# A hybrid state-space and attention block: squares added feature-major, Toeplitz taps from SBUF, bias tiles that stay

## The chip, the cores and the metric

The kernel runs on one core of one Trainium2 chip. The metric is the device time of one execution in microseconds (us), as the median of several runs. A core has a matrix engine (PE; its weight loads are listed apart, as PEld), a vector engine (DVE), a scalar engine (ACT), a general-purpose engine (POOL) and a sync engine (SP) which here only issues transfers. The engines run their own instruction queues in order and wait for each other through semaphores. Sixteen DMA engines move data between DRAM and SBUF, the on-chip memory; PE writes its products into PSUM, eight banks from which the other engines read.

## What is computed

The input is x, 2048 tokens by 1024 features, in float32. The reference, cut to what the change touches:

```python
h = rmsnorm(x, norm_mix_g)              # x * rsqrt(mean(x*x, over features) + eps) * g
proj = h @ w_in                         # 1024 -> 512 (u) + 512 (q) + 512 (k) + 512 (v)
# group A: 32 channel groups of 16, one 64-dim diagonal complex state each
lam_bar = exp(lam * dt);  b_bar = ((lam_bar - 1) / lam)[..., None] * b_mat
states = scan(a_r * b_l + b_r over time, b_bar applied to u)
y_ssm = Re(C states) + d_skip * u;  y_ssm = glu(gelu(y_ssm))
# group B: 8 heads of 64; each 64-frame chunk looks at itself and the 8 chunks before
idx = clip(rel, -128, 128) + 128;  bias = rel_bias[:, idx]
out = softmax(q k^T / 8 + bias, invalid chunks at -1e30) @ v
x = x + concat(rmsnorm(y_ssm), rmsnorm(out)) @ w_out
x = x + (silu(h2 @ w_gate) * (h2 @ w_up)) @ w_down          # h2 = rmsnorm(x)
return rmsnorm(x)
```

Three things in it matter below. The normalisation of the first projection needs, for each token, the sum of its squared features. The recurrence of group A is done in stretches of 8 time steps: inside a stretch it is a small Toeplitz matrix, whose entries ("taps", Re(C lam_bar^k B) for k = 0..7, with d_skip added at k = 0) are made from the parameters inside the kernel. The bias of a head depends on the distance alone, so a tile of 128 query rows by 640 keys is one row of 768 values, shifted by one per query row, with two 64 by 64 corners that mark keys out of reach.

## The kernel before

The program runs through five phases: a first stage (`u_phase`), attention with the state-space units woven in (`att_phase`, `ssm_unit`), the output projection (`mix_phase`), and the feed-forward layer (`gate_up_phase`, `down_phase`). Products are made to float32 accuracy from float32r halves: an operand is split into a rounded part `hi` and a rest `lo`, and each product is three matmuls (`mm3`).

**First stage.** It computes u = h @ w_in[:, :512] in four blocks of 512 tokens, in the order 1, 2, 3, 0 (`BLOCKS`); we call these turns n = 0 to 3. For each block `prep` loads eight feature-major tiles `xt` of 128 features by 512 tokens (L441, four buffers), makes `hi` on ACT (L443, with the gain folded in) and `lo` on DVE (L444). It then loads the same tokens once more, token-major, as four tiles of 128 by 1024 (L450), and ACT squares each and adds along its row (L451); the four sums per token tile go to a Newton iteration on DVE (`newton`, L102 to L113, thirteen small instructions), started in `sums`. A `group` is one output tile of 128 features by 512 tokens: 24 matmuls. The scale of block n-1 is applied in turn n behind its first group: `finish` spreads the reciprocal roots over the partitions with PE (`spread_`, eight matmul records into a PSUM bank called `pp`), ACT copies them out (L473, L477, L478), DVE multiplies the four held groups (L483) and POOL sends them to DRAM (L484). A held group keeps its PSUM bank until then.

**The state-space prologue.** `ssm_prologue` is a generator; `long(n)` in `u_phase` advances it n steps, and `LONG = 1, 3, 2` says how many in each turn. It computes powers of lam_bar and b_bar, then four pieces `v` on DVE (L283 to L287), each of which POOL sends to DRAM (L345) with its state rows for the two channel groups of a pair lying in different halves of the 128 partitions. The other operand goes to DRAM as well (`bb`, L335). Both are read back regrouped, so that real and imaginary part of one channel group fill the 128 partitions (`bbg` L372, `vg`/`v` L379, 512 KB each), and 32 matmuls over 128 rows (L389) give the taps, four matmuls per PSUM bank; ACT copies them out (L390), DVE adds the diagonal (L392), POOL writes them to `kts` (L393). A chain of small complex multiplications on POOL (L356 to L365) makes the powers `a8`, `sw` for the scan. Last come 32 transposes of `wt` (L289 to L298), whose results ACT copies out (L295) and POOL sends to DRAM (`bsts`). These last parts are yielded into the first attention projection.

**Attention.** The phase is a list of 128 steps which a planner fills with the projection work of later blocks. The first step needs q and k of head pair 0 (`qk(0,0)`, 48 matmuls), made ready by ACT, DVE and a copying transfer (L750, L751). Each step multiplies q and k into a PSUM tile `sc`, DVE adds the bias tile `nb` and takes the row maximum in one instruction (L830), ACT takes the exponential, PE transposes the result (`pt`) and multiplies it with v. Bias tiles come from a DRAM array `nbm` of 8 heads by 128 by 640, built once by one 2.56 MB transfer and two transfers for the corners (L522, L525); `load_nb` (L799 to L802) loads one head's tile into one of two buffers. A state-space unit loads its operands `U`, `Bst`, `Tm`, `Vm` in 18 transfers (L550), multiplies on PE (`pj`), and scans on POOL.

All `dma_start` calls written `nc.sync` stand in SP's queue, those written `nc.gpsimd` in POOL's; a queue issues in program order, so a transfer whose semaphore wait is not fulfilled holds back the ones after it. In SP's queue each issue also waits until the transfer eight places earlier has landed, as there are eight semaphores in turn.

Of the kernel before, what the change touches and what calls it, by code (L numbers as in the profile page):

```python
# [65 lines left out]
LONG = 1, 3, 2  # L66
# [91 lines left out]
def ssm_prologue(k, ident, S):  # L158
# [3 lines left out]
    with tc.tile_pool(name="pro", bufs=1) as p:  # L162
# [126 lines left out]
        def transposes(b_, wt):  # L289
            bst = k.t(p, "v" if b_ > 1 else "vg", [P, 9 if b_ > 1 else 8, 2, NS], bufs=2)[:, :8]  # L290
# [46 lines left out]
        wts = []  # L337
        for b_ in range(4):
            qs = slice(4 * b_, 4 * b_ + 4)
# [27 lines left out]
        kt = k.t(p, "kt", [CH, 8, P], bufs=2)  # L367
        nc.gpsimd.memset(kt[:], 0.0)
        for b_ in range(4):
            nc.gpsimd.dma_start(S["kt"][:, 8 * b_ : 8 * b_ + 8, 0], kt[:])  # L370
        bb = k.t(p, "bbg", [P, NG, CH])
        nc.sync.dma_start(bb[:], S["bb"].rearrange("q g c n m -> (c n) (q g) m"))  # L372
        dm = k.t(p, "cm1", [P, 576])[:CH, : NG * CH].rearrange("c (g m) -> c g m", g=NG)
        V.tensor_tensor(dm, ident[:CH, :CH].unsqueeze(1).to_broadcast([CH, NG, CH]),
                        ddt[:].unsqueeze(2).to_broadcast([CH, NG, CH]), op=ALU.mult)
        vgs = []
        for b_ in range(4):
            vgs.append(k.t(p, "vg", [P, 8, P], bufs=2)[:] if b_ < 2 else k.t(p, "v", [P, 9, P], bufs=2)[:, :8])
            nc.sync.dma_start(vgs[b_], S["v"].rearrange("q g c n m -> (c n) (q g) m")[:, 8 * b_ : 8 * b_ + 8, :P])  # L379
        for b_ in range(4):  # L380
            gs = slice(8 * b_, 8 * b_ + 8)
            vg = vgs[b_]
            kt = k.t(p, "kt", [CH, 8, P], bufs=2) if b_ < 2 else k.t(p, ("bc", "small")[b_ - 2], [CH, 8, P])
            if b_ == 0:
                yield
            for g0 in (0, 4):
                ps = k.t(k.pro_psum, "pp", [P, 512])[:].rearrange("p (a b) -> p a b", a=4)
                for g in range(4):
                    k.te.matmul(ps[:CH, g, :], bb[:, 8 * b_ + g0 + g, :], vg[:, g0 + g, :], start=True, stop=True)  # L389
                nc.scalar.copy(kt[:, g0 : g0 + 4, :], ps[:CH])  # L390
                yield
            V.tensor_tensor(kt[:, :, :CH], kt[:, :, :CH], dm[:, gs], op=ALU.add)  # L392
            nc.gpsimd.dma_start(S["kt"][:, gs, 1], kt[:])  # L393
# [4 lines left out]
def u_phase(k, ident, S, aw):  # L398
# [3 lines left out]
    with ExitStack() as cx:  # L402
        p1 = cx.enter_context(tc.tile_pool(name="u1", side="right", bufs=1))
        p2 = cx.enter_context(tc.tile_pool(name="u2", side="right", bufs=2))
        p3 = cx.enter_context(tc.tile_pool(name="u3", side="right", bufs=4))
        psum = cx.enter_context(tc.tile_pool(name="ups", bufs=4, space=bass.MemoryType.PSUM, reuse_waits="tile"))
# [23 lines left out]
        def prep(b, each=None):  # L430
            X[b] = operands(b)
            for q in range(KT):
# [11 lines left out]
                nc.vector.scalar_tensor_tensor(lo, xt[:], k.gm[:, q : q + 1], f32(hi), op0=ALU.mult, op1=ALU.subtract)  # L444
                if each:
                    each(q)
            ST[b] = ss = k.t(p2, "ss", [P, 4])
            for i in range(4):
                xn = next(xns)
                nc.sync.dma_start(xn, io["x"][b * SB + i * P : b * SB + (i + 1) * P])  # L450
                nc.scalar.activation(xn, xn, AF.Square, accum_out=ss[:, i : i + 1])  # L451
# [87 lines left out]
        long(7 - sum(LONG))  # L539
    return pro, att  # L540

# [122 lines left out]
def att_phase(k, ident, S, aw, x0, roots):  # L664

    tc, nc, io, pfs = k.tc, k.nc, k.io, k.pfs
    with ExitStack() as cx:
# [129 lines left out]
        nbs = {}  # L797
# [886 lines left out]
```

## Time and profile before

| | |
|---|---|
| median of three runs (lowest, highest) | 2352.8 us (2351.67, 2358.15) |
| profiled execution: its time as the profile has it, span | 2352.2 us |
| PE busy | 2204.0 us, 94% |
| DVE / ACT / POOL busy | 1468.7 / 1001.3 / 1136.5 us |
| first stage, first matmul to last spread | 7.4 to 115.5 us |
| first projection for attention, first scores, second step | 115.5, 141.6, 158.7 us |
| mean granted TensorE clock | 0.970 of full speed |

The page has no time of the profiled execution other than its span; the span lies 0.6 us below the median of the runs. In the rows, "L79" is the line of the one function that issues all matmuls, so matmuls are told apart by the names of their output and inputs ("ps<-hi,wuh"), and "pf", "ps" and "pp" are PSUM banks. Several tiles of the first stage carry the name of a buffer used for weights later (raw, w, xt, hi0x): they are halves of those buffers, borrowed. A row of the timeline has its start, its length, engine, line, operation, names, a count of like instructions in a row, and in brackets how long the engine had been idle before and what released it. A matmul in float32 appears as two records. Matmuls overlap in the pipeline, so a distance between starts tells more than a length.

### The profile page before, as it was taken

How to read it: one execution, taken by the hardware profiler on the slowest of the kernel's cores; microseconds unless marked ns; L12 is line 12 of the kernel's file. 1: busy time of each engine (PE TensorE's matmuls, PEld its weight loads, DVE VectorE, ACT ScalarE, POOL GpSimd, SP SyncE). 2: the span in 40 equal slices, each digit the busy share in tenths (PEclk: the TensorE clock that was granted, in tenths of full speed). 3: DMA queues.
4: the chain of work that ended last, by engine and by line, in shares of the span. 5: the costliest groups of instructions: out<-in, count | busy, mean ns of one | idle time of the engine just before them, and what ended most of it. 6: DMA issues, size and time to landing. Idle time of an engine off the chain costs nothing.

```text
span 2352.2 us, 30719 instructions
## 1 busy us (share of the span) xinstructions
PE 2204.0 (94%) x10712; PEld 1853.1 (79%) x10712; DVE 1468.7 (62%) x2229; ACT 1001.3 (43%) x1666; POOL 1136.5 (48%) x1280
## 2 busy tenths in 40 slices
PE   8977799999997899989999998999999989999996
PEld 6766688898986788768888887788888868888886
DVE  6745645656555855746775668766645365579676
ACT  4435545555546642333333334433333343345332
POOL 3237644356551432465555557655555364345442
PEclk9989999999998999989999999999999989999998
DMA  8967776776644434743554646554423287465551
GB/s 275 299 203 251 213 205 178 206 213 189 187 139 135 157 117 148 264 143 117 188 171 157 231 169 243 191 199 165 170 89 119 75 310 261 169 211 184 204 179 72
DMA packets 225331, 434.92 MB, mean 185 GB/s; under 512 B 43480, under 2 KB 70152, under 8 KB 218072
## 3 DMA queue, kind: packets, MB, share of 16 engines
q1 hardware_dynamic: 220312, 418.79, 54.1%
q0 software_dynamic: 4864, 14.17, 2.0%
q8 instruction: 84, 1.38, 0.2%
q14 instruction: 71, 0.58, 0.1%
HBM read 292.88 MB, written 132.15 MB: 181 GB/s over the span
## 4 chain that ended last, share of the span: by engine, by line
PE 57%; DVE 4%; issue 1%; DMA 1%; POOL 1%; ACT 1%; SPq 0%; DVEq 0%; ACTq 0%; POOLq 0%
PE X L79 19%; PE ps L79 17%; PE Y L79 9%; PE big L79 7%; PE W L79 5%; DVE sa L1527 1%; DVE lo L155 1%; DMA lo<-hc 0%; POOL c L155 0%; POOL lo L155 0%; POOL sa L1098 0%; DVE hd L155 0%; DMA hd<-wc 0%; DVE S L1346 0%; ACT hi L155 0%
## 5 line engine op out<-in xcount | busy, mean ns | idle before, releaser
L79 PE MATMUL X<-hi,c 128*128 128x512 f32 x1408 | 450.4, 390 | 8.0 <-POOL c L155 4.0
L79 PE MATMUL ps<-hd,hd 128*128 128x512 f32 (+1 forms) x1968 | 435.1, 384 | 8.0 <-DVE hd L155 4.5
L79 PEld LDWEIGHTS ps<-hd,hd 128*128 128x128 f32 x1968 | 361.4, 191 | 80.4 <-DVE hd L155 4.9
L155 POOL TENSOR_TENSOR c<-S,c 128x512 fp32r<-128x512 f32 x176 | 252.8, 1438 | 245.2 <-ACT c L155 242.9
L79 PEld LDWEIGHTS X<-hi,c 128*128 128x128 f32 x1408 | 264.9, 188 | 65.5 <-POOL c L155 4.4
L155 POOL TENSOR_TENSOR hd<-hd 128x1536 fp32r<-128x1536 f32 (+1 forms) x53 | 188.2, 3556 | 211.2 <-ACT hd L155 196.0
L79 PE MATMUL X<-lo,c 128*128 128x512 f32 x704 | 274.4, 390 | 0.0
L155 POOL TENSOR_TENSOR c<-raw,c 128x512 fp32r<-128x512 f32 x132 | 188.1, 1425 | 130.6 <-ACT c L155 100.1
L155 ACT CAST hd<-hd 128x1536 fp32r<-128x1536 f32 (+1 forms) x106 | 147.3, 1392 | 227.6 <-DMA hd<-hq 162.8
L79 PE MATMUL Y<-hi,c 128*128 128x512 f32 x704 | 228.1, 395 | 14.1 <-DVE u L1368 14.1
L1492 DVE TENSOR_TENSOR acc<-acc,ps 128x512 f32<-128x512 f32 x196 | 129.2, 682 | 89.9 <-PE ps L79 89.8
L79 PEld LDWEIGHTS Y<-hi,c 128*128 128x128 f32 x704 | 134.1, 190 | 44.0 <-DVE u L1368 15.8
L830 DVE CUSTOM_DVE_ANT_0 s<-sc,nb 128x640 f32<-128x640 f32 (+4 forms) x128 | 94.5, 738 | 115.7 <-PE sc L79 104.5
L588 POOL TENSOR_TENSOR st<-X,a 128x128 f32<-128x128 f32 (+2 forms) x136 | 46.7, 343 | 247.2 <-ACT X L574 237.1
L79 PE MATMUL big<-m,woh 128*128 128x512 f32 x512 | 163.5, 401 | 0.2 <-DVE yr L1034 0.2
L79 PE MATMUL pf<-hi,w 128*128 128x512 f32 x416 | 151.8, 416 | 9.0 <-ACT w L155 4.6
L155 ACT CAST c<-S 128x512 fp32r<-128x512 f32 x176 | 109.3, 621 | 114.0 <-PE Y L79 59.5
L79 PEld LDWEIGHTS X<-lo,c 128*128 128x128 f32 x704 | 132.4, 188 | 27.3
L1364 ACT COPY u<-X 128x512 f32<-128x512 f32 x132 | 77.0, 584 | 180.2 <-PE X L79 180.2
L155 ACT CAST c<-raw 128x512 fp32r<-128x512 f32 x132 | 82.1, 622 | 152.6 <-PE Y L79 83.0
L79 PE MATMUL Y<-lo,c 128*128 128x512 f32 x352 | 138.4, 393 | 0.0
L155 DVE TENSOR_TENSOR hd<-hd 128x1536 fp32r<-128x1536 f32 (+1 forms) x53 | 111.6, 2107 | 34.3 <-ACT hd L155 33.9
(450 smaller groups left out, 4701.4 us busy)
## 6 DMA issues: line engine op xcount, KB each, us to landing
w<-wss SPq DMA_DIRECT2D x36, 1024.0 KB, 5.6
hq<-g SPq DMA_DIRECT2D x140, 256.0 KB, 2.1
hd<-hq SPq DMA_DIRECT2D x42, 768.0 KB, 4.5
hd<-wc SPq DMA_DIRECT2D x42, 768.0 KB, 6.1
raw<-in_w_gate SPq DMA_DIRECT2D x44, 512.0 KB, 3.7
raw<-in_w_up SPq DMA_DIRECT2D x44, 512.0 KB, 4.1
wc<-px SPq DMA_DIRECT2D x66, 256.0 KB, 3.1
wss<-w SPq DMA_DIRECT2D x12, 1024.0 KB, 5.9
```

Source lines behind the costliest of these rows:

```text
L79: return self.tc.keep_in_program_order(self.tc.nc.tensor.matmul(*a, **b))
L155: return nc.scalar.copy(hi, raw), (lo_eng or nc.gpsimd).tensor_tensor(lo, raw, f32(hi), op=ALU.subtract)
L588: eng.tensor_tensor(t[:, :, :, :n], src, ar, op=ALU.mult)
L830: nc.vector.tensor_tensor_reduce(s[:, :nk].rearrange("p (a b) -> p a b", a=nch), ps[:, :nch, :half], hd.nb[:, nk - 1 :: -1].rearrange("p ( ...
L1364: nc.scalar.copy(u[:], ps[:])
L1492: V.tensor_tensor(a, a, ps[:], op=ALU.add)
L1527: (nc.gpsimd if m else nc.vector).tensor_tensor(self.sa[m][:, :n], self.sa[m][:, :n], t[:, :n], op=ALU.add)
```

## The change

Three parts of the first stage and its surroundings are exchanged.

1. *Squares.* The token-major loads of x go (16 transfers of 512 KB), and so do the 16 squares with row sums on ACT. Each feature-major tile `xt` is now also squared on ACT (128 by 512, 32 in all), and POOL adds the eight squares of a block into one tile (seven adds per block, each on the one before). `sums` multiplies that tile with a vector of ones on PE (`tok_sums`, four matmuls, eight records) into a `pp` bank, which `newton` reads. `sums` stands behind the last group of a turn for n < 3, and ahead of it for n = 3; the squares have two buffers, so a square waits for the add two before.
2. *Taps.* `bb`, its writes and `bbg`, and the four reads of `vg`/`v` go. The `v` transfers to DRAM stay, since the state-space units read them. The taps are 16 matmuls of 64 rows each per quarter instead of 8 of 128 rows: the two halves of the partitions hold the two channel groups of a pair, real and imaginary part add up in PSUM, and the two halves write two PSUM banks in turn. A table `LONGS` says which of `outputs` (v), `inputs` (wt) and `taps` each step of the prologue makes; the taps come between the groups of turns n = 2 and n = 3 instead of inside `qk(0,0)`, the transposes move into `qk(0,0)`, and the `bsts` transfers stand in POOL's queue between the instructions of the `a8` chain.
3. *Bias.* `nbm`, its 2.56 MB transfer and its two corner transfers go. Two tiles of 128 by 640 last for the whole attention phase, one made in the first stage (`nba`, its corners set by POOL, its rows loaded in turn n = 1) and one at the start of attention (`nbb`). `load_nb` fills a tile by two transfers of 64 by 576 straight from the 768-value rows; the corners are not touched again. There are 64 such transfers instead of 32 of 128 by 640.

In the program as built, the `newton` of turn 0 stands on DVE behind the third `lo` of turn n = 2 and ends behind the sixth; that of turn 1 lies between the fourth and the sixth `lo` of turn 3. The rows of `nbb` stand in SP's queue ahead of the first `U` loads, and wait for the landing of the first two `bsts` transfers, because `nbb` lies where their tiles lay.

```diff
-LONG = 1, 3, 2
+VO, WI, TA = range(3)
+LONGS = ((VO, 0),), ((VO, 1),), ((TA, 0), (VO, 2)), ((TA, 1), (VO, 3)), ((TA, 2), (WI, 0)), ((TA, 3), (WI, 1)), ((WI, 2),), ((WI, 3),)
...
-            bst = k.t(p, "v" if b_ > 1 else "vg", [P, 9 if b_ > 1 else 8, 2, NS], bufs=2)[:, :8]
+            bst = (k.t(p, "v", [P, 9, 2, NS], bufs=2) if b_ < 2 else k.t(p, ("bc", "small")[b_ - 2], [P, 8, 2, NS]))[:, :8]
...
-        for g2 in range(2):
-            for c, bt in ((0, bbr), (1, bbi)):
-                nc.gpsimd.dma_start(S["bb"][:, g2, c].rearrange("q n m -> n q m"), bt[g2 * NS : (g2 + 1) * NS])
+        dm = k.t(p, "dm", [CH, NG, CH])
+        V.tensor_tensor(dm[:], ident[:CH, :CH].unsqueeze(1).to_broadcast([CH, NG, CH]),
+                        ddt[:].unsqueeze(2).to_broadcast([CH, NG, CH]), op=ALU.mult)
...
+        def taps(b_):
+            kt = k.t(p, "kt", [CH, 8, P], bufs=2)
+            gs = slice(8 * b_, 8 * b_ + 8)
+            pss = [k.t(k.pro_psum, "pp", [P, 512])[:].rearrange("p (a b) -> p a b", a=4) for _ in range(2)]
+            for q in range(4):
+                for c, bt in enumerate((bbr, bbi)):
+                    for g2, ps in enumerate(pss):
+                        rows = slice(g2 * NS, (g2 + 1) * NS)
+                        k.te.matmul(ps[:CH, q, :], bt[rows, 4 * b_ + q, :], vts[b_][c][rows, q, :L, :].rearrange("p k c -> p (k c)"), start=c == 0, stop=c == 1)
+            for g2, ps in enumerate(pss):
+                nc.scalar.copy(kt[:, g2::2, :], ps[:CH])
+            V.tensor_tensor(kt[:, :, :CH], kt[:, :, :CH], dm[:, gs], op=ALU.add)
+            nc.gpsimd.dma_start(S["kt"][:, gs, 1], kt[:])
...
+        for make in LONGS:
+            for m, b_ in make:
+                (outputs, inputs, taps)[m](b_)
             yield
...
-        bb = k.t(p, "bbg", [P, NG, CH])
-        nc.sync.dma_start(bb[:], S["bb"].rearrange("q g c n m -> (c n) (q g) m"))
...
-        vgs = []
-        for b_ in range(4):
-            vgs.append(k.t(p, "vg", [P, 8, P], bufs=2)[:] if b_ < 2 else k.t(p, "v", [P, 9, P], bufs=2)[:, :8])
-            nc.sync.dma_start(vgs[b_], S["v"].rearrange("q g c n m -> (c n) (q g) m")[:, 8 * b_ : 8 * b_ + 8, :P])
-        for b_ in range(4):
-            gs = slice(8 * b_, 8 * b_ + 8)
-            vg = vgs[b_]
-            kt = k.t(p, "kt", [CH, 8, P], bufs=2) if b_ < 2 else k.t(p, ("bc", "small")[b_ - 2], [CH, 8, P])
-            if b_ == 0:
-                yield
-            for g0 in (0, 4):
-                ps = k.t(k.pro_psum, "pp", [P, 512])[:].rearrange("p (a b) -> p a b", a=4)
-                for g in range(4):
-                    k.te.matmul(ps[:CH, g, :], bb[:, 8 * b_ + g0 + g, :], vg[:, g0 + g, :], start=True, stop=True)
...
+        p4 = cx.enter_context(tc.tile_pool(name="u4", side="right", bufs=2))
...
+                sq = k.t(p4, "sq" if q else "sa", [P, SB])
+                nc.scalar.activation(sq[:], xt[:], AF.Square)
+                if q:
+                    nc.gpsimd.tensor_tensor(ST[b][:], ST[b][:], sq[:], op=ALU.add)
+                else:
+                    ST[b] = sq
                 if each:
                     each(q)
-            ST[b] = ss = k.t(p2, "ss", [P, 4])
-            for i in range(4):
-                xn = next(xns)
-                nc.sync.dma_start(xn, io["x"][b * SB + i * P : b * SB + (i + 1) * P])
-                nc.scalar.activation(xn, xn, AF.Square, accum_out=ss[:, i : i + 1])
...
         def sums(b):
+            ps = k.t(psum2, "pp", [P, SB])
+            tok_sums(k, te, ps, 0, ST[b])
             with tc.high_priority():
-                ST[b] = newton(k, p2 if b else aw, ST[b][:], D, 4)
+                ST[b] = newton(k, p2 if b else aw, ps[:, :4], D, 4)
...
             if n == 1:
-                corner = k.t(p1, "corner", [64, 64])
-                nc.gpsimd.memset(corner[:], 1e30)
-                nc.sync.dma_start(S["nbm"][:], bass.AP(S["nb"].tensor, S["nb"].offset + 1, [[768, H], [1, P], [1, 640]]))
-            if n == 3:
-                for m in range(2):
-                    corners = nc.sync.dma_start(S["nbm"][:, m * 64 : m * 64 + 64, m * 576 : m * 576 + 64].rearrange("h p c -> p h c"), corner[:].unsqueeze(1).to_broadcast([64, H, 64]))
-                    tc.keep_in_program_order(corners)
+                bias_corners(k, S["nba"])
+                bias_rows(k, S, 0, S["nba"])
             pf = FBANKS[n]
             now = [group(b, 0, 0 in pf)]
             finish(last, held)
-            long(LONG[n - 1])
+            long(1)
             if n == NSB - 1:
                 att = att_phase(k, ident, S, aw, X[b], lambda: ST[b])
                 next(att)
-                long(1)
-            now += [group(b, f, f in pf) for f in (1, 2)]
-            sums(b)
+            for f in (1, 2):
+                now.append(group(b, f, f in pf))
+                if n > 1:
+                    long(1)
+            if n == NSB - 1:
+                sums(b)
             held = now + [group(b, 3, 3 in pf)]
+            if n < NSB - 1:
+                sums(b)
...
+def bias_corners(k, nb):
+    for m in range(2):
+        k.nc.gpsimd.memset(nb[m * 64 : m * 64 + 64, m * 576 : m * 576 + 64], 1e30)
+def bias_rows(k, S, h, nb):
+    src = bass.AP(S["nb"].tensor, S["nb"].offset + h * 768 + 65, [[1, 64], [1, 576]])
+    k.nc.sync.dma_start(nb[:64, 64:], src)
+    k.nc.sync.dma_start(nb[64:, :576], src)
+    return nb
...
-        nbs = {}
+        nbs = {0: S["nba"]}
         def load_nb(h):
-            nb = k.t(aa, "nb", [P, 640], bufs=2)
-            nc.sync.dma_start(nb[:], S["nbm"][h])
-            return nb
+            return bias_rows(k, S, h, nbt[h % 2])
...
+        nbt = S["nba"], k.t(aa, "nbb", [P, 640])
+        bias_corners(k, nbt[1])
```

More of the change, by code (lines that the diff above doesn't have):

```diff
@@ L346, in ssm_prologue, with inputs @@
                                       vt[c][g2 * NS : (g2 + 1) * NS].rearrange("n q k c -> n q (k c)"))
-            yield
-        for b_ in range(4):
+            vts.append(vt)
+        def inputs(b_):
             qs = slice(4 * b_, 4 * b_ + 4)
@@ L365, in ssm_prologue @@
             G.tensor_copy(S["sw"][:, n, 1, :], a8[:, 1, :, e])
[L367 to L393 removed]
+        yield
         for b_ in range(4):
@@ L533, in u_phase @@
                 next(att)
-                long(1)
-            now += [group(b, f, f in pf) for f in (1, 2)]
-            sums(b)
+            for f in (1, 2):
[4 more added lines that the diff above has]
+                sums(b)
             held = now + [group(b, 3, 3 in pf)]
+            if n < NSB - 1:
+                sums(b)
         finish(b, held)
-        long(7 - sum(LONG))
+        long(1)
     return pro, att
+def bias_corners(k, nb):
[6 more added lines that the diff above has]
+    return nb
 def ssm_unit(k, p, psum, S, b, eng):
@@ L1593, in block_kernel @@
             "ya": k.t(dram, "ya_s", [NSB, DS, SB]), "x1": k.t(dram, "x1", [D, SEQ]),
-            "k": k.t(dram, "ks", [2, H, P, SB]), "nbm": k.t(dram, "nbms", [H, P, 640]), "nb": k.t(dram, "nbs", [H, 768]),
+            "k": k.t(dram, "ks", [2, H, P, SB]), "nb": k.t(dram, "nbs", [H, 768]),
             "bst": k.t(dram, "bsts", [4, P, 8 * P]), "v": k.t(dram, "vs", [NPR, 2, 2, NS, 9 * CH]),
@@ L1597, in block_kernel @@
             "hq": k.t(dram, "hq", [2, F2, 7, P, 512]), "wc": k.t(dram, "wc", [F2, 7, P, 512]), "wt": k.t(dram, "wt", [4, P, HALF]),
-            "bb": k.t(dram, "bbs", [NPR, 2, 2, NS, CH]), "kt": k.t(dram, "kts", [CH, NG, 2, P]),
+            "kt": k.t(dram, "kts", [CH, NG, 2, P]),
         }
@@ L1618, in block_kernel @@
             S["sw"] = k.t(p, "sw", [P, 3, 2, NPR])
+            S["nba"] = k.t(p, "nba", [P, 640])
             with tc.tile_pool(name="apf", bufs=2, space=bass.MemoryType.PSUM, reuse_waits="tile") as k.pfs:
```

8 lines of the change are left out of this document (6 added, 2 removed).

## The prediction

> **What bounds the kernel now.** I read the page's totals and the chain of waits first, then the stretches of the first 180 us, PE's timeline there, and the waits of the same stretch.
>
> ```profile
> span 2352.2 us, 30719 instructions
> PE 2204.0 (94%) x10712; PEld 1853.1 (79%) x10712; DVE 1468.7 (62%) x2229; ACT 1001.3 (43%) x1666; POOL 1136.5 (48%) x1280
> PE 57%; DVE 4%; issue 1%; DMA 1%; POOL 1%; ACT 1%; SPq 0%; DVEq 0%; ACTq 0%; POOLq 0%
> ```
>
> PE is busy 94% of the span and carries the chain, so a microsecond counts when it comes off PE's queue: a gap on PE or work of PE. The change touches only the first 180 us, apart from the later bias loads. The stretches (columns: length, busy us of each engine with its instructions, granted clock, DMA share, GB/s):
>
> ```profile
> 0.00:60.00 60.00, 49.94 (x194) 38.27 (x195) 41.12 (x188) 28.10 (x43) 17.80 (x36) 0.94 0.82 276
> 60.00:120.00 60.00, 55.72 (x244) 44.01 (x243) 46.44 (x92) 25.38 (x39) 12.30 (x22) 0.97 0.90 297
> 145.40:158.70 13.30, 0.04 (x2) 0.04 (x1) 0.78 (x3) 0.59 (x2) 0.00 (x0) 0.60 1.02 333
> 400.00:500.00 100.00, 95.55 (x576) 85.25 (x575) 63.30 (x110) 55.10 (x107) 60.63 (x160) 0.98 0.69 210
> ```
>
> From 400 us on PE is at 95%, so time won before it should reach the end. Ahead of it PE stands still for 13.3 us in one stretch in which the DMA engines are full (1.02). The waits say why, and PE's timeline gives the points I measure from:
>
> ```profile
> PE sc L79 <- DVE mn L830: 13.3, 1, 13.3
> DVE s L830 <- DMA nb<-nbms: 9.8, 1, 9.8
> ACT raw L443 <- DMA xt<-in_xp: 14.6, 1, 14.6
> ```
>
> ```profile
> 31.38 0.39 PE L79 MATMUL pf<-hi,wuh 128*128 128x512 f32 x1
> 43.00 1.91 PE L79 MATMUL pp<-ident,no 128*128 128x128 f32 x8
> 64.73 0.50 PE L79 MATMUL ps<-raw,wuh 128*128 128x512 f32 x1 [3.08 <-ACT raw L443]
> 74.80 1.05 PE L79 MATMUL pp<-ident,no 128*128 128x128 f32 x8
> 114.73 1.05 PE L79 MATMUL pp<-ident,no 128*128 128x128 f32 x8
> 115.53 0.48 PE L79 MATMUL pf<-hi,w 128*128 128x512 f32 x1
> 119.82 1.92 PE L79 MATMUL pp<-vg,bbg 128*16 128x128 f32 x16
> 121.67 0.50 PE L79 MATMUL pf<-hi,w 128*128 128x512 f32 x1
> 134.83 1.47 PE L82 MATMUL pp<-ident,wt 128*128 128x128 f32 x12
> 138.31 2.93 PE L82 MATMUL pp<-ident,wt 128*128 128x128 f32 x20 [2.01 <-ACT vg L295]
> 141.63 0.33 PE L79 MATMUL sc<-hi2x,hi0x 128*128 128x128 f32 x1 [0.39 <-ACT v L295]
> 145.16 0.28 PE L79 MATMUL pf<-w,lo 128*128 128x256 f32 x1
> 158.69 0.55 PE L79 MATMUL sc<-hi2x,hi0x 128*128 128x256 f32 x1 [13.26 <-DVE mn L830]
> 161.76 0.40 PE L79 MATMUL pf<-w,hi 128*128 128x256 f32 x2
> 163.06 0.28 PE L79 MATMUL pf<-w,lo 128*128 128x256 f32 x1
> 177.50 1.89 PE L79 MATMUL pj<-U,Bst 128*128 128x256 f32 x8
> ```
>
> There are three losses: the bias tile that arrives late (13.26 us), the third block's late `xt` (3.08 us and a slow run to 74.80), and 4 x 1.85 us of taps (121.67 - 119.82) on PE inside the first attention projection. The span is 2352.2 us, the median of the runs 0.6 above it; I add 0.6 at the end.
>
> **Part 1, squares.** What goes and what comes has these rows (for the tile view: lowest, median and highest ns):
>
> ```profile
> w<-in_x SPq DMA_DIRECT2D x16, 512.0 KB, 6.9
> xt<-in_xp SPq DMA_DIRECT2D x32, 256.0 KB, 5.7
> L451 ACT ACTIVATE w<-w 128x1024 f32<-128x1024 f32 x16 | 17.0, 1060 | 10.3 <-DMA w<-in_x 9.0 <-DVE small L199 1.1
> L443 ACT ACTIVATE hi<-xt,g_mix 128x512 fp32r<-128x512 f32 x16 | 10.9, 714 | 7.8 <-DMA xt<-in_xp 7.8
> L444 DVE SCALAR_TENSOR_TENSOR lo<-xt,g_mix,hi 128x512 fp32r<-128x512 f32 x16 | 11.9, 748 | 2.1 <-ACT hi L443 2.1
> L987 DVE TENSOR_TENSOR sq<-sq,sg x16: 678/686/1769, 740.7 to 918.0; 128x512 f32<-128x512 f32 x16
> L983 ACT ACTIVATE sq<-ya x4: 613/615/630, 737.1 to 873.2; 128x512 f32<-128x512 f32 x4
> L1098 POOL TENSOR_TENSOR sa<-sa,xt 128x512 f32<-128x512 f32 x16 | 23.4, 1463 | 24.8 <-ACT xt L1094 23.9
> L79 PE MATMUL big<-ones,sq 128*128 128x1 f32 x56 | 7.0, 245 | 1.1 <-DVE nv L105 1.1
> 21.18 0.72 ACT L443 ACTIVATE hi2x<-xt,g_mix 128x512 fp32r<-128x512 f32 x1 [0.87 <-DMA xt<-in_xp]
> ```
>
> 16 x 512 KB leave SP's queue and the DMA engines. ACT's 16 x 1.06 = 17 us become 32 x 0.62 = 20 us, still far below its span. POOL gets 28 x 1.46 = 41 us in the first 100 us, where it has been idle three quarters of the time (17.8 + 12.3 of 120 us busy). Behind an add that waits stand, in POOL's queue, the `u` transfers, the prologue's `v` transfers and the `a8` chain; `u` is wanted only by the state-space units, and `a8` by their scan, far later. On ACT a square waits for the add two before, and the next `hi` stands behind it: that is why the pace of adds enters below. PE gets 8 records per block at 7.0 / 56 = 0.125 us, 1.0 us per block, on the path. So block 0's matmuls end at 31.4 as now, its token sums at 32.4, and turn 1's first group (24 x 0.227 = 5.45 us, now with no waits for `xt`) at 37.9, where it was 43.0.
>
> Then PE needs the spread, and so `newton`, which stands on DVE behind the `lo` tiles of two turns to come (its last instructions behind the 14th tile after block 0's). The pace of a tile is the add, 1.46, or the cycle of the four `xt` buffers, (5.7 + 0.71 + 0.75) / 4 = 1.8; I take 1.6. From 21.18 + 0.72 + 0.62 = 22.5, 14 tiles end at 44.9, the root some 0.6 later: the spread at 45.5, a wait of 7.6 us that isn't there today. Today's rows show an idle PE running slow when it resumes: from 158.69 to 161.76 14 matmuls took 3.07 us, the next twelve 1.43. I put 1.4 us on it. Turn 1 ends at 45.5 + 0.8 + 3 x 5.45 + 1.4 = 64.0, its token sums at 65.0, turn 2's first group at 70.5, since the late `xt` wait should go with half the traffic. The second `newton` stands behind turn 3's `lo` tiles and I give it 1.5 us: spread at 72.0 instead of 74.8. Bounds of this part: from 4.3 won (the second wait gone) to 1 lost.
>
> **Part 2, taps.** From the spread at 74.80 to the last at 114.73 PE has 39.93 us with no gap. This stays, with two token sums (2.0) and four taps added: the last spread at 113.9 + 4 T. T lies between 1.92 (the row of the same product: as many multiply-adds, 16 records) and 3.84 (32 records at the same 0.12 each). I take 1.92, the row of the same product, since two halves of 64 rows fill the array as one of 128 did: 121.6 (at 3.84: 129.3).
>
> [...]
>
> The projection now takes 134.83 - 115.53 = 19.3 less 7.4 of taps, plus 4.4 - 0.3 = 4.1 for the transposes that move into it: it ends 0.8 + 16.0 after the spread. From its end to the first scores I keep today's 141.63 - 134.83 = 6.8, as the copying transfers of the halves take that long with or without the transposes. First scores at 121.6 + 23.6 = 145.2.
>
> The DRAM round trip goes for nothing on the path: SP loses five issues, POOL four, and the rows of 119.82 show no wait for what they bring. The four `kts` writes stand earlier in POOL's queue, and PE's taps would wait for `v` from DVE (4.5 us a quarter, six rows like L444's 0.75); two turns of 22 us hide that. If that cover were gone, it would cost 4.5 us each.
>
> **Part 3, bias.** Head 0's tile is there long before. The second step follows after today's work alone, 145.4 - 141.6 = 3.8: at 149.0 instead of 158.7. That is 9.7 us, and 1.4 more for the slow restart.
>
> What is late next is the state-space operands:
>
> ```profile
> 148.86 10.65 SPq L550 DMA_DIRECT2D U<-u  x8
> U<-u SPq DMA_DIRECT2D x8, 64.0 KB, 8.8
> bsts<-v POOLq DMA_DIRECT2D x2, 512.0 KB, 13.1
> ```
>
> Today they are issued from 148.86 and are needed at 177.50. Now they stand behind `nbb`, which waits for the first two `bsts` to land. With the transposes in the projection these are issued about 11 us after the spread and land 13.1 later, then come 10.65 of issue and 8.8 of landing: 44 after the spread. `pj` comes 23.6 + 3.8 + 18.8 = 46 after it. A slack of 2 us, against 9 today, is worth a charge of 2 (0 to 7). Later bias loads are 64 instead of 32 with less data and prefetched a head ahead: I charge nothing, by the stretch at 400 us, where the DMA share is 0.69. The corners are two small fills on POOL, ahead of `nbb`'s rows; they add to the same lateness.
>
> Sum: 9.7 + 1.4 - 2 = 9.1 us; 2352.2 - 9.1 + 0.6 = 2343.7, say 2344.
>
> **Rivals.** (a) The 64-row halves run one after the other. Price 4 x 1.92 = 7.7 us on PE: 2351.5, no change. For it: every matmul row shows 128 rows, none shows overlap of halves.
>
> (b) Slower: DVE and POOL get in each other's way, and DVE becomes the first stage's limit. DVE has 41 + 46 of 120 us already. The row of L987 on DVE runs to 1.77 us at a median of 0.69, while POOL works beside it; a collision thus costs 1.08. With 28 adds, 28 x 1.08 = 30 us of DVE time, and it decides once 15 of them (16 us, the 9 gained and 7 more) fall on the path; with 17 the time is 2344 + 18 = 2362. Against it: DVE's idle 33 us can take up many.
>
> [...]
>
> (c) The waits for `newton` don't come: with half the traffic `xt` lands in 3 us, PE reaches the spreads a little ahead only. Six of the 7.6 us and the 2 of `U` come back: 2336.
>
> (d) The change doesn't do what it says for the time: the bias wait is replaced by one for `U` and `Bst` at its bound, 7 us instead of 2: 2349, no change. For it: the slack of 2 us.
>
> **How the numbers follow.** Forecast 0.40, (a) 0.22, (b) 0.20, (c) 0.13, (d) 0.05. Faster is forecast and (c): 0.53; same (within 0.3%, 7 us, about what a measurement tells from no change) is (a) and (d): 0.27; slower 0.20. The range runs from 2333 (beyond (c)'s middle) to 2361 (about the upper half of (b) left out); the likeliest case alone spans 2340 to 2348.
>
> **What would show it.** Right: PE waits at the first spread until about 45, no wait at L830 for `nb`, the last spread near 122, 32 records of taps in 1.9 us, second step near 149, `pj` near 168. Wrong: taps of 3.8 us, POOL adds beyond 2 us with DVE instructions stretched beside them, PE waiting at each spread, or a long gap before `pj`.

## The result, and the profile after

The changed kernel takes 2383.0 us (median of four runs, 2377.1 to 2386.5) against 2352.2 before (median of four runs beside it): a ratio of 1.0129, 95% interval 1.0108 to 1.0151. It is slower by 31 us; 2344 was predicted, with a range up to 2361. The profiled execution has a span of 2384.5 us. The page's totals and its chain of waits for the changed kernel:

```profile
span 2384.5 us, 30951 instructions
PE 2219.1 (93%) x10808; PEld 1867.1 (78%) x10808; DVE 1509.9 (63%) x2229; ACT 1001.2 (42%) x1666; POOL 1175.3 (49%) x1307
PE 56%; DVE 4%; issue 2%; POOL 2%; DMA 1%; ACT 1%; SPq 0%; DVEq 0%; POOLq 0%; ACTq 0%
```

DVE executes as many instructions as before, 2229, and is busy for 41 us more (1509.9 against 1468.7). Its rows have grown longer. The first two stretches, with the columns as before, and PE's waits in the first 250 us (total, times, longest), show where PE lost its time:

```profile
0.00:60.00 60.00, 34.63 (x128) 25.11 (x128) 51.86 (x132) 34.89 (x57) 37.65 (x41) 0.86 0.55 160
60.00:120.00 60.00, 53.35 (x276) 43.78 (x277) 50.11 (x112) 15.79 (x25) 29.80 (x38) 0.88 0.44 130
```

```profile
PE pp L80 <- DVE no L114: 19.0, 3, 14.5
PE pf L80 <- DVE lo L448: 5.0, 4, 2.3
```

In the first 60 us PE works 34.6 us instead of 49.9, while the DMA share fell from 0.82 to 0.55, as intended. The granted clock of PE is lower too, 0.86 and 0.88 in the two stretches against 0.94 and 0.97; what this adds to the loss was not separated. What PE waits for is DVE: 19.0 us for the last instruction of `newton` (L114), 5.0 us for `lo` tiles. On PE's timeline the points that the prediction set come out so:

```profile
33.76 0.95 PE L80 MATMUL pp<-ones,sa 128*128 128x1 f32 x8
62.90 2.08 PE L80 MATMUL pp<-ident,no 128*128 128x128 f32 x8 [14.54 <-DVE no L114]
92.51 2.05 PE L80 MATMUL pp<-ident,no 128*128 128x128 f32 x8 [3.75 <-DVE no L114]
146.85 1.13 PE L80 MATMUL pp<-ident,no 128*128 128x128 f32 x8 [0.67 <-DVE no L114]
166.53 0.45 PE L80 MATMUL sc<-hi2x,hi0x 128*128 128x128 f32 x1 [4.04 <-DVE hi2x L775]
174.14 0.28 PE L80 MATMUL sc<-hi2x,hi0x 128*128 128x256 f32 x1
191.57 1.89 PE L80 MATMUL pj<-U,Bst 128*128 128x256 f32 x8
```

The last spread is at 146.85, 32.1 us later than before; some 7.4 us of this are the four quarters of taps, which stood behind it before. The second step is at 174.14, 15.5 us later, so 16.7 us are won between these two points. After that the gap to the kernel before grows again. Each of the 128 attention steps has one bias addition on DVE; the 33rd starts 24.1 us later than before (333.3 against 309.3), the 65th 19.4 (482.3 against 462.9), the last 26.4 (first row before, second row changed):

```profile
755.93 0.81 DVE L830 CUSTOM_DVE_ANT_0 s<-sc,nb 128x640 f32<-128x640 f32 x1
782.37 0.81 DVE L849 CUSTOM_DVE_ANT_0 s<-sc,nbb 128x640 f32<-128x640 f32 x1
```

The rest of the program adds another 6 to the difference of the two spans, 32.3.

**What happened at the first spread.** DVE's timeline (some of the short instructions of the root, and a `lo` tile between them) and POOL's, for the same twelve microseconds of the changed kernel; the last two rows are two of the six adds shown singly:

```profile
50.83 0.15 DVE L106 TENSOR_SCALAR nv<-pp 128x4 f32<-128x4 f32 x1
51.30 1.24 DVE L108 TENSOR_SCALAR nf<-nf 128x4 f32<-128x4 f32 x1
54.01 1.78 DVE L448 SCALAR_TENSOR_TENSOR w<-xt,g_mix,w 128x512 fp32r<-128x512 f32 x1
55.71 1.22 DVE L113 TENSOR_TENSOR nf<-nf,nv 128x4 f32<-128x4 f32 x1
57.02 1.25 DVE L114 SCALAR_TENSOR_TENSOR no<-nf,ny 128x4 f32<-128x4 f32 x1
60.41 1.22 DVE L114 SCALAR_TENSOR_TENSOR ny<-nf,no 128x4 f32<-128x4 f32 x1
62.70 0.15 DVE L114 SCALAR_TENSOR_TENSOR no<-nf,ny 128x4 f32<-128x4 f32 x1
```

```profile
51.25 8.38 POOL L452 TENSOR_TENSOR sa<-sa,sq 128x512 f32<-128x512 f32 x6 [5.94 <-ACT sa L450]
60.20 1.41 POOL L452 TENSOR_TENSOR sa<-sa,sq 128x512 f32<-128x512 f32 x1 [0.56 <-ACT sq L450]
51.25 1.26 POOL L452 TENSOR_TENSOR sa<-sa,sq 128x512 f32<-128x512 f32 x1 [5.94 <-ACT sa L450]
56.98 1.26 POOL L452 TENSOR_TENSOR sa<-sa,sq 128x512 f32<-128x512 f32 x1
```

An instruction on 128 by 4 elements takes 0.15 us when POOL is idle (50.83) and up to 1.25 us when it meets an add (57.02). Where it is held by one, it ends with the add: the instruction of 51.30 ends at 52.54, the add of 51.25 at 52.51; that of 57.02 at 58.27, the add of 56.98 at 58.24. Between two adds in a row one DVE instruction or a few get through (three, started from 52.45 to 52.61, ahead of the next one held). The root, fourteen instructions of 0.15 each (the program has fourteen, not thirteen), needs from 50.83 to 62.85, twelve microseconds. Three `lo` tiles and short instructions of the prologue stand between them; in the kernel without the adds (`no_add`, below) the same sequence needs 5.1 us, from 35.58 to 40.72.

### The profile page after: what moved, and what is told of

It reads as the page before. It is cut to its first block, busy times and chain, and to the rows that moved or that the text cites. A ratio compares the mean times of both kernels' runs of the same rounds, so it can differ in the third digit from the quotient of the medians.

```text
span 2384.5 us, 30951 instructions
## 1 busy us (share of the span) xinstructions
PE 2219.1 (93%) x10808; PEld 1867.1 (78%) x10808; DVE 1509.9 (63%) x2229; ACT 1001.2 (42%) x1666; POOL 1175.3 (49%) x1307
## 4 chain that ended last, share of the span: by engine, by line
PE 56%; DVE 4%; issue 2%; POOL 2%; DMA 1%; ACT 1%; SPq 0%; DVEq 0%; POOLq 0%; ACTq 0%
PE X L80 19%; PE ps L80 17%; PE Y L80 9%; PE big L80 6%; PE W L80 5%; DVE sa L1548 1%; DMA lo<-hc 1%; DVE lo L156 1%; POOL lo L156 1%; POOL c L156 0%; DVE hd L156 0%; POOL sa L1119 0%; DMA hd<-wc 0%; DVE S L1367 0%; DVE acc L1565 0%
## 5 line engine op out<-in xcount | busy, mean ns | idle before, releaser
L80 PEld LDWEIGHTS X<-lo,c 128*128 128x128 f32 x704 | 133.0, 189 | 27.4
L868 DVE TENSOR_TENSOR ptl<-pt,pth 128x640 fp32r<-128x640 f32 (+3 forms) x152 | 98.3, 647 | 46.9 <-ACT pth L867 45.1
```

What stands on the lines that cost most here:

```text
L80: return self.tc.keep_in_program_order(self.tc.nc.tensor.matmul(*a, **b))
L868: nc.vector.tensor_tensor(ptl[:, a:b, qp, :], pt[:, a:b, :], f32(pth[:, a:b, qp, :]), op=ALU.subtract)
```

## The experiments

Besides the changed kernel eleven others ran, one of them in two sets of runs. The kernel before ran beside each set (its medians: 2351.7 to 2354.1 us), and the ratios are to those runs, so differences of medians from different sets are good to 2 or 3 us only. Part 1 alone on the kernel before was not tried; its effect is read from kernels with and without it. The measured times:

| kernel | median us (runs) | ratio to before, 95% |
|---|---|---|
| changed: parts 1, 2, 3 | 2383.0 (4) | 1.0129, 1.0108 to 1.0151 |
| sq_before: parts 2 and 3 | 2343.9 (6) | 0.9965, 0.9951 to 0.9979 |
| no_add: changed, without the adds | 2349.6 (10) | 0.9997, 0.9983 to 1.0012 |
| dve_add: changed, adds on DVE | 2357.6 (10) | 1.0020, 1.0008 to 1.0032 |
| taps_only: part 2 | 2340.0 (4) | 0.9952, 0.9936 to 0.9968 |
| taps_more: part 2, again | 2343.2 (6) | 0.9954, 0.9942 to 0.9966 |
| bias_only: part 3 | 2341.7 (6) | 0.9953, 0.9938 to 0.9969 |
| bias_before: parts 1 and 2 | 2371.3 (4) | 1.0072, 1.0048 to 1.0096 |
| nb_halves: part 2, tiles in two loads | 2350.8 (10) | 0.9991, 0.9978 to 1.0005 |
| idle_adds: part 2 and 28 adds for nothing | 2358.8 (10) | 1.0020, 1.0006 to 1.0033 |
| whole_tiles: parts 2 and 3, one load per tile | 2344.1 (12) | 0.9970, 0.9957 to 0.9984 |
| halves_act: parts 2 and 3, half the loads on ACT | 2354.1 (12) | 1.0004, 0.9991 to 1.0017 |
| taps_seq: part 2, halves one after the other | 2349.9 (1) | one run |

**Which part loses: the squares.** My theory was that POOL's adds hold DVE up; rivals were that the moved taps and transposes lose, and that the root is late because it stands behind the `lo` tiles. The kernels `sq_before`, `taps_only`, `no_add` and `dve_add` separate them. In `sq_before` part 1 is undone:

```diff
-                sq = k.t(p4, "sq" if q else "sa", [P, SB])
-                nc.scalar.activation(sq[:], xt[:], AF.Square)
-                if q:
-                    nc.gpsimd.tensor_tensor(ST[b][:], ST[b][:], sq[:], op=ALU.add)
-                else:
-                    ST[b] = sq
...
+            ST[b] = ss = k.t(p2, "ss", [P, 4])
+            for i in range(4):
+                xn = next(xns)
+                nc.sync.dma_start(xn, io["x"][b * SB + i * P : b * SB + (i + 1) * P])
+                nc.scalar.activation(xn, xn, AF.Square, accum_out=ss[:, i : i + 1])
```

> The changed kernel with part 1 (squares) put back to that of the kernel before; taps and bias as changed. Theory 1 (POOL's adds lock DVE out: small DVE instructions of 0.17 us take 1.3 us beside an add): without the adds DVE's rows are back at 0.17 and 0.75 us, the first spread is at about 43, the last near 121, and the time is 2336 to 2348. Theory 2 (the loss comes from the taps between the groups, the moved transposes and the later bias tile): the loss stays, 2370 to 2383.

Measured: 2343.9 us, and the time of the kernel before is beaten by 0.35%. The first spread is at 38.66 and the last at 113.45, both earlier than expected. Part 1 costs 39.1 us (2383.0 - 2343.9) with part 3 there and 28 to 31 without it (2371.3 - 2343.2 and - 2340.0). The theory that the taps lose falls here, and once more with `taps_only`, in which parts 1 and 3 are undone (the edit above, and the bias as before):

> The kernel before with part 2 (taps from SBUF, transposes inside the first projection) alone; squares and bias as before. By theory 1 the taps cost PE what they cost before (32 records at half the distance), so the gain is small: the late bias tile stays and takes back what the moved transposes win. 2346 to 2354. Theory 2 (taps and moved transposes are the loss): 2362 or more.

Measured: 2340.0, better than the 2346 to 2354 expected; the gain is taken up below.

In `no_add` only the last square of a block is summed, and everything else of part 1 stays:

```diff
-                if q:
-                    nc.gpsimd.tensor_tensor(ST[b][:], ST[b][:], sq[:], op=ALU.add)
-                else:
+                if q in (0, KT - 1):
                     ST[b] = sq
```

> The changed kernel without the 28 adds on POOL: only the last square of a block enters the sums, so the scale is not that of the reference. ACT's squares, the token sums on PE and the place of the root behind later tiles stay. Theory 1 (lock): DVE rows unstretched, first spread between 40 and 47, time 2340 to 2352. Theory 3 (the root is late since it stands behind the lo tiles of two turns, paced by ACT and by the landing of xt): first spread still at 55 or later, time 2370 or more.

Measured: 2349.6, with the first spread at 40.87. DVE's order is the same in both kernels: the root ends behind the 22nd `lo` tile, 14 tiles after block 0's last. From the start of the 8th to that of the 22nd it is 18.6 us here (21.34 to 39.90) and 32.8 in the changed kernel (29.24 to 62.04). So the place of the root in DVE's queue costs next to nothing by itself; the theory of the place falls, and with it my 7.6 us. The groups of DVE's short instructions in the first 125 us say the same (one row before, the next two of the changed kernel, the last of `no_add`; columns: busy us, mean ns, idle before):

```profile
L187 DVE TENSOR_SCALAR small<-small 128x16 f32<-128x16 f32 x13 | 2.2, 172 | 0.0
```

```profile
L188 DVE TENSOR_SCALAR small<-small 128x16 f32<-128x16 f32 x13 | 5.3, 419 | 0.0
L114 DVE SCALAR_TENSOR_TENSOR no<-nf,ny 128x4 f32<-128x4 f32 x6 | 4.0, 664 | 0.1
```

```profile
L188 DVE TENSOR_SCALAR small<-small 128x16 f32<-128x16 f32 x13 | 2.1, 169 | 0.0
```

and, on PE's timeline of `no_add`, the first spread:

```profile
40.87 1.13 PE L80 MATMUL pp<-ident,no 128*128 128x128 f32 x8 [1.74 <-DVE small L195]
```

The same instruction means 172 ns before, 419 in the changed kernel, and 169 with the adds gone. Over the whole program DVE is busy 1468.9 us in `no_add` and 1509.9 in the changed kernel; the difference, 41.0, is nearly what the 28 adds take on POOL, 40.6 (28 x 1.45). What is left of part 1 without the adds, 5.8 us (2349.6 - 2343.9), was not looked into further.

In `dve_add` the adds move to DVE:

```diff
-                    nc.gpsimd.tensor_tensor(ST[b][:], ST[b][:], sq[:], op=ALU.add)
+                    nc.vector.tensor_tensor(ST[b][:], ST[b][:], sq[:], op=ALU.add)
```

> The changed kernel with the 28 adds on DVE instead of POOL. Theory 1 (lock): DVE gets 28 x 0.69 = 19 us of work but no stretched rows; first spread at 46 to 52, time 2345 to 2365. Theory 3 (pace of ACT and landings, or mere amount of work beside lo): as changed or slower, 2375 to 2395.

Measured: 2357.6, with the first spread at 43.58, earlier than expected. DVE has 28 instructions more (2257) and is busy 27 us less (1482.7), and the kernel is 25 us faster than with POOL helping. It is still 14 us behind token-major squares.

**Waiting for the sum, or being held up?** In `idle_adds` part 2 stands alone, squares are token-major, and POOL makes 28 adds which no one reads:

```diff
+        scr = k.t(p1, "scr", [P, SB])
+        nc.gpsimd.memset(scr[:], 0.0)
...
+                if q:
+                    nc.gpsimd.tensor_tensor(scr[:], scr[:], f32(hi), op=ALU.add)
```

> The kernel with part 2 alone, and 28 adds of 128 by 512 on POOL that nothing waits for, each behind one hi tile. The output is unchanged. Theory 1 (an add locks DVE out for its whole length): small DVE rows of 1.2 to 1.4 us appear again beside the adds, the first spread moves from 43 to 48 or later, and the time is 2348 to 2365. Rival (the loss comes from waiting for the adds' results): 2338 to 2343, DVE rows unstretched.

Measured: 2358.8, 15.6 to 18.8 us more than without these adds (2343.2 and 2340.0). PE's, DVE's and POOL's timelines of this kernel, and behind them the first spread and the start of the root in `taps_only`:

```profile
42.63 0.80 PE L80 MATMUL pf<-lo,wuh 128*128 128x512 f32 x1 [6.37 <-DVE lo L449]
55.06 1.35 PE L80 MATMUL pp<-ident,no 128*128 128x128 f32 x8
39.99 0.15 DVE L106 TENSOR_SCALAR nv<-ss 128x4 f32<-128x4 f32 x1
46.24 0.15 DVE L114 SCALAR_TENSOR_TENSOR no<-nf,ny 128x4 f32<-128x4 f32 x1
46.69 3.53 DVE L449 SCALAR_TENSOR_TENSOR lo<-xt,g_mix,hi 128x512 fp32r<-128x512 f32 x2
50.14 1.50 DVE L284 TENSOR_TENSOR cm<-small,bc 128x256 f32<-128x256 f32 x1
46.70 4.66 POOL L451 TENSOR_TENSOR scr<-scr,hi 128x512 f32<-128x512 f32 x3 [5.35 <-ACT hi L448]
```

```profile
43.24 1.78 PE L80 MATMUL pp<-ident,no 128*128 128x128 f32 x8
30.12 0.17 DVE L106 TENSOR_SCALAR nv<-ss 128x4 f32<-128x4 f32 x1
```

From 46.70 to 51.36 POOL adds three times, and in that time DVE gets two `lo` tiles and one product done, 5.0 us for what takes 0.75 + 0.75 + 0.41 without POOL. The first spread is at 55.06 instead of 43.24 in `taps_only`. Here PE waits not for the root, which is done at 46.39, but for the `lo` tiles of its first group (6.37 us ahead of 42.63): DVE reaches the start of the root at 39.99 instead of 30.12, as the adds of the first 25 us already held it up. The view of their tile `scr` names no one who waited for the adds, so these 16 to 19 us are lost by holding up alone, on whichever DVE result PE needs next. In the changed kernel the adds cost 33 us (2383.0 - 2349.6). There the root and the next squares also wait for their results, which I take to be the rest; this was not shown by itself, and the two were measured on different squares.

What holds DVE up beside an add no trace shows; what they show is the length. In the first 100 us of the changed kernel 20 rows of 4 or 16 columns are held by an add of L452: they take 1.12 to 1.32 us and end 0.02 to 0.04 us behind it.

**Taps.** The kernels with part 2 have the 32 records of a quarter at half the distance of the 16 before (1.86 us in `taps_only` from the first record to the matmul behind the quarter, against 1.85 for 16 before), but for one: in `taps_seq` the same matmuls come one half of the partitions after the other:

```diff
-            for q in range(4):
-                for c, bt in enumerate((bbr, bbi)):
-                    for g2, ps in enumerate(pss):
+            for g2, ps in enumerate(pss):
+                for q in range(4):
+                    for c, bt in enumerate((bbr, bbi)):
```

> The kernel with part 2 alone, the taps of one half of the partitions all ahead of those of the other half. If two matmuls of 64 rows run beside each other only when they lie in different halves and stand next to each other, the 32 records of a quarter take 3.4 to 3.8 us instead of 1.8 and the time is 6 to 8 us up; if 64 rows cost half in any order, they stay at 1.8.

PE's timeline of `taps_only`, the first and the last rows of one quarter and the matmul behind it, and of `taps_seq`, the first rows, one from the middle, the last rows of one and the matmul behind it:

```profile
79.86 0.40 PE L80 MATMUL pp<-v,bbr 64*16 64x128 f32 x4
81.40 0.39 PE L80 MATMUL pp<-v,bbi 64*16 64x128 f32 x4
81.72 0.73 PE L80 MATMUL pf<-raw,wuh 128*128 128x512 f32 x2
```

```profile
82.36 0.39 PE L80 MATMUL pp<-v,bbr 64*16 64x128 f32 x2
83.68 0.40 PE L80 MATMUL pp<-v,bbr 64*16 64x128 f32 x4
84.79 0.38 PE L80 MATMUL pp<-v,bbi 64*16 64x128 f32 x2
85.23 0.38 PE L80 MATMUL pp<-v,bbi 64*16 64x128 f32 x2
85.53 0.73 PE L80 MATMUL pf<-raw,wuh 128*128 128x512 f32 x2
```

In 0.22 us four records start in the one and two in the other; only in the middle, where the second half follows the first, four start here too. From the first record to the matmul behind the quarter it is 1.86 us in turn (81.72 - 79.86) and 3.17 one half after the other (85.53 - 82.36): 1.3 us a quarter, 5.2 in all. The speed comes from the order, not from 64 rows as such; the expected 3.4 to 3.8 was a little high. The one run's time, 2349.9, is too little to hold more.

**Bias.** `bias_only` is part 3 alone on the kernel before, `bias_before` the changed kernel with the tiles of before (`load_nb` with one 128 by 640 transfer from `nbm`):

> The kernel before with part 3 (bias tiles filled in halves) alone. The second step no longer waits for its tile, so attention starts 8 to 13 us earlier. If the later loads are harmless the time is 2339 to 2344; if they cost as much as the difference of the two runs with and without part 3 says (2343.9 against 2340.0, although attention starts 8 us earlier with it), 11 to 15 us of the head start go again by 320 us and the time is 2350 to 2356.

> The changed kernel with the bias tiles of before; squares on POOL and taps as changed. If the adds on POOL are the loss and part 3 costs some 10 us in the attention phase, the first spread stays at 60 to 65 and the time is 2368 to 2378; if part 3 is harmless, 2382 to 2390.

Measured: 2341.7 and 2371.3. In `bias_only` the second step is at 141.01, 17.7 us earlier than before, more than expected; 15.0 us of this are left at the last bias addition. The first spread of `bias_before` is at 58.47, a little ahead of the range expected. So part 3 wins 11 us alone, and loses 11.7 in the changed kernel (2383.0 - 2371.3) and some 1 to 4 beside part 2 (2343.9 against 2340.0 and 2343.2). The reason that the gains of parts 2 and 3 do not add up lies in the wait of 13.26 us which both were to deal with. In `taps_only` the bias tile is loaded from `nbm` as before, yet the second step does not wait for it:

```profile
142.08 0.44 PE L80 MATMUL sc<-hi2x,hi0x 128*128 128x128 f32 x1 [4.02 <-DVE hi2x L762]
150.04 0.41 PE L80 MATMUL sc<-hi2x,hi0x 128*128 128x256 f32 x1
```

The view of the tile `nb` in `taps_only` names no one who waited for it; its transfers land so (lowest, median, highest us):

```profile
DMA to landing us min/median/max: 3.0/4.3/10.1
```

Before, its first landing took 12.9 us while the DMA engines were full (a share of 1.02 from 145.4 to 158.7). Part 2 takes the reads of `vg` and `bbg` away and issues `bsts` earlier, which I take to be the reason; it was not tested by itself. Either way each part alone removes the wait, and it can be removed once.

That leaves a loss in part 3. `nb_halves` is part 2 with each tile from `nbm` in two transfers:

```diff
-            nc.sync.dma_start(nb[:], S["nbm"][h])
+            nc.sync.dma_start(nb[:64], S["nbm"][h, :64])
+            nc.sync.dma_start(nb[64:], S["nbm"][h, 64:])
```

> The kernel with part 2 alone, each bias tile loaded from the same DRAM array in two transfers of 64 rows. If the number of issues in SP's queue is what part 3 costs, 2346 to 2352 against 2340.0; if it is something else (the overlapping source, the place in the queue), 2338 to 2343.

Measured: 2350.8, 10.7 us more than `taps_only` and 7.6 more than `taps_more`. SP's timeline shows one place of the loss, in the `xt` loads of a later token block (first `taps_only`, then `nb_halves`):

```profile
221.76 0.33 SPq L704 DMA_DIRECT2D xt<-in_xt  x1
224.34 3.63 SPq L643 DMA_DIRECT2D y<-X  x8
```

```profile
228.71 3.60 SPq L643 DMA_DIRECT2D y<-X  x8
240.09 0.38 SPq L558 DMA_DIRECT2D Vm<-vs  x1
241.11 0.38 SPq L704 DMA_DIRECT2D xt<-in_xt  x1
```

With the extra issue the third `xt` load stands behind the state-space unit's output stores, which wait 8.6 us for ACT, and is issued 12 us after them instead of ahead of them. PE's waits in the attention phase for the tiles made from such loads (`hi`) are 7.5 us here, 4.0 in `taps_only` and 8.4 in `sq_before` (whose profiled execution took 2354.8 us, 11 more than its median). This is not the whole of the 7.6 to 10.7. Two versions tried to keep what part 3 wins. `whole_tiles` loads a tile by one transfer from the 768-value rows and lets DVE set the corners each time; `halves_act` issues the second half from ACT's queue:

```diff
-    k.nc.sync.dma_start(nb[:64, 64:], src)
-    k.nc.sync.dma_start(nb[64:, :576], src)
+    k.nc.sync.dma_start(nb[:], bass.AP(S["nb"].tensor, S["nb"].offset + h * 768 + 1, [[1, P], [1, 640]]))
+    for m in range(2):
+        k.nc.vector.memset(nb[m * 64 : m * 64 + 64, m * 576 : m * 576 + 64], 1e30)
```

```diff
-    k.nc.sync.dma_start(nb[64:, :576], src)
+    k.nc.scalar.dma_start(nb[64:, :576], src)
```

> Parts 2 and 3 with squares as before, and each bias tile loaded straight from the 768-value rows by one transfer of 128 by 640, its two corners set by DVE behind the landing (two fills of 64 by 64 per tile). If the second transfer per tile is what takes the head start away, attention starts near 136 as with both parts, the start is kept, and the time is 2328 to 2337. If it is the overlapping source or the place of the loads, 2341 to 2346.

> Parts 2 and 3 with squares as before; the second half of each bias tile is issued from ACT's queue, so SP's queue has as many bias loads as before. If SP's queue is what part 3's second transfer costs, the head start of some 20 us at the first scores is still 12 or more at the end: 2332 to 2340. If ACT's queue pays for it, or the cost is not in SP's queue, 2341 to 2350.

(`taps_more` is `taps_only` once more; the kernel above is `halves_act`.)

> The kernel with part 2 alone, once more in more rounds beside the one above, since the earlier four runs give a wide interval: 2338 to 2343. If parts 2 and 3 both remove the same wait, the late first bias tile, neither this nor the kernel above is ahead of the other by more than 4 us.

Measured: 2344.1, 2354.1 and 2343.2. In its profiled execution (span 2334.4) `whole_tiles` keeps its head start over `taps_more` (4.2 us at the first bias addition, 4.9 at the last), and PE's wait for `hi` is 4.0 us; but its runs spread from 2336.5 to 2352.7, and their median is that of `sq_before`. As a time this is inconclusive. `halves_act` is slower than either range expected, and 10.9 us behind `taps_more`, where 4 was the most. It starts attention like `sq_before` and, in an execution of 2361.4 us, is 14.6 us behind `taps_more` at the last bias addition, 12 of them lost behind the 73rd. So moving the issue to another queue does not save it.

The traces of all kernels say the same about the second transfer. From the second step (the first matmul of `sc` with 256 columns) to the last bias addition it is 586.0 to 597.2 us in the seven kernels that load a tile in one transfer (before, both with part 2 alone, `taps_seq`, `idle_adds`, `bias_before`, `whole_tiles`) and 598.2 to 614.9 in the seven that load it in two. `whole_tiles` (592.1, one execution) reads the same overlapping source as part 3, which speaks against the source as the cost; `halves_act` (614.9) shows that it is not SP's queue alone. In which waits the whole price lies stays open.

No version beats `taps_only`, `taps_more` and `bias_only` by more than the runs spread. Parts 2 and 3 each make a kernel that beats both the one before and the changed one, by 0.46 to 0.48% against the one before.

## Why the prediction was wrong

**Wrong: the pace of the tiles ahead of the root.** The step that failed is the pace of a `lo` tile ("I take 1.6"), counted from 22.5, which gave "the root some 0.6 later: the spread at 45.5". It booked POOL's adds at 1.46 us (1.45 measured, L452) and DVE's instructions at their lengths with POOL idle. Measured: the last tile of block 0 starts only at 29.24, the 14 tiles behind it take 2.3 us each, and the spread is at 62.90, a wait of 14.5 us instead of 7.6. DVE, whose spare time was to hide the adds, is busy for 28.9 of the 29.1 us between 33.8 and 62.9. With the adds gone the same instructions in the same order take 1.3 us a tile, the spread is at 40.87 and the wait 1.7 us, so what I had weighed, the place of the root behind 14 tiles, costs next to nothing. Of the 25.2 us by which the last spread missed its forecast (146.85 against 121.6), 17.4 stand at the first spread, 3.1 come up to the second (92.51 against 72.0) and 4.7 after it.

**Wrong: the chance and the price of rival (b).** It named what happened, one add holding DVE for 1.08 us. Measured at the first spread, a short instruction that is held by an add loses just that, 1.07 to 1.10 (1.22 to 1.25 against 0.15). With 28 x 1.08 = 30 us of DVE time it was too low (41.0 measured), and its 2362 is 21 us short of 2383.0. "DVE's idle 33 us can take up many" was the wrong bound: DVE was idle after the places where PE needed it. The slower side had 0.20, and the range ended at 2361.

**Wrong: "I charge nothing" for the later bias loads.** They cost 7.6 to 10.7 us when each tile is loaded in two transfers (`nb_halves`), and in the changed kernel 11.7 with all of part 3 (against `bias_before`). The DMA share I cited does not speak of waits in a queue.

**Right, but not to be had twice: part 3's 9.7 us.** The second step follows 7.6 us behind the first scores (166.53 to 174.14) without a wait for a tile. Part 2 removes this wait too, which the sum did not see.

**Right: part 2.** T = 1.86 us against 1.92 taken. That two halves of 64 rows take the time of one of 128 was my assumption, as the kernel before has no matmul of 64 rows; the runs showed that time for halves in turn (1.86 us, `taps_only`) and not for one half after the other (3.17, `taps_seq`), the order that rival (a) would need. From the last spread to the first scores it is 19.7 us instead of the forecast 23.6, and from there to the second step 7.6 instead of 3.8. The sum of the two, 27.3 against 27.4, is right by luck. **Right: no cost of the state-space operands**: `pj` follows at 191.57 without a wait. Rivals (c) and (d) did not occur.

The sum as measured, against the kernel before at the same points: 32.1 us lost up to the last spread, 16.7 won from there to the second step, and 17 lost behind it: 11 in the attention phase (15.5 late at its second step, 26.4 at its last) and 6 after it. The 11 go with part 3: `bias_before`, the same kernel without it, takes 592.3 us for the same stretch, where the changed kernel takes 608.2 and the kernel before 597.2. The 6 have no cause that I know; from the last bias addition to the end, where nothing was changed, the fourteen traces lie between 1596.3 and 1606.2 us, so they may be scatter.

## What to carry to other kernels

Work moved to POOL was not free for DVE here: 28 adds of 128 by 512, together 40.6 us on POOL, made DVE busy for 41.0 us more. Price such adds at up to their own length of DVE time where DVE has work, above all where a chain of short instructions ends in a PE wait (14.5 us at the first spread). Before parts of a change are added up, look whether they remove the same wait. A transfer more per step can cost time though no byte is added: here 32 more transfers of half the size cost 7.6 to 10.7 us.

## What the runs showed of the hardware

In the changed kernel a DVE instruction on 4 or 16 columns that takes 0.15 to 0.17 us takes 1.12 to 1.32 when it is held by a POOL add of 128 by 512 (1.26 to 1.60 us, one of 3.85), and ends 0.02 to 0.04 us behind it; in all, 28 adds of together 40.6 us made DVE busy for 41.0 us more (against `no_add`). A TENSOR_SCALAR with one tensor as input was held (1.24 us, L108) as was a TENSOR_TENSOR with two (1.22, L113). Matmuls over 64 rows in different halves of the partitions, one after the other in turn and into two PSUM banks, started up to twice as densely as those within one half: four records in 0.22 us against two, and 32 in 1.86 us (`taps_only`) against 3.17 (`taps_seq`).
